# A mixer block with its input projection moved to the front and done by seven products per unit

## The chip, the cores and the metric

One core of one Trainium2 chip runs the whole program. The metric is the time of one execution in device microseconds. The core's engines are named as the profile names them: PE (TensorE, matrix products), PEld (its loading of stationary operands), DVE (VectorE), ACT (ScalarE), POOL (GpSimd) and SP (SyncE, which issues nearly all transfers here). Each engine takes its own instructions in order.

## What is computed

One layer of a decoder trunk on 1024 positions of 1024 features, in float32, batch 1. One projection `z = rms_norm(x) @ w_in` of 13312 columns feeds three branches and three gates; each branch has its own output projection, is multiplied by its gate, and the sum goes through `w_out` and then an MLP of 4096 features.

```python
h = rms_norm(x, g_mix)
rq, rk, rv, rg, dq, dk, dv, cq, gates = split_cols(h @ w_in, SPLITS)   # 1024,1024,2048,2048,1024,1024,1024,1024,3072
ret    = swish(rg) * head_norm(retention(rq, rk, rv), g_ret, True)     # 4 heads, chunks of 128
da     = head_norm(diff_attention(dq, dk, dv, lam), g_diff, False) * (1 - lam_init)   # 4 heads, two softmax maps
kv     = rms_norm(mem, g_mem) @ w_mem_kv                               # 256 memory tokens
ca     = memory_cross_attention(cq, kv)                                # 4 heads
g      = sigmoid(gates)
merged = g[0] * (ret @ w_ret_o) + g[1] * (da @ w_diff_o) + g[2] * (ca @ w_cross_o)
x = x + merged @ w_out
x = x + relu(rms_norm(x, g_ffn) @ w_up) ** 2 @ w_down
return rms_norm(x, g_final)
```

## The kernel before

Everything large lies with features on partitions and positions along the free axis, in two halves of 512 positions (`t` = 0, 1). Each operand of a product is kept as a high and a low part in float32r (`split`, lines 132 to 134: ACT casts, DVE subtracts), and `mm3` (lines 142 to 147) adds three matmuls for one product of blocks. `fm_gemm` (line 233) multiplies a block of 128 columns of a weight with one half of the normalised `hT`: 8 blocks of features, 24 matmuls of 512 columns, called a **half** here. Values are projected with positions on partitions, in tiles of 256 columns, 24 matmuls each.

The program goes through these stages, written one after another; a scheduler keeps each engine's order close to the written one. x comes in quarters, is normalised, and three gate blocks are multiplied on the way (`first_gemm`, line 330). Then memory keys and values (lines 377 to 399). Cross attention (lines 402 to 480) projects its queries head by head. Differential attention (lines 506 to 665) projects queries, keys and values of a head and then runs eight steps over blocks of 128 queries, from the longest (i = 7) to the shortest: scores (tile `dsc`), a DVE instruction that adds the bias and takes the maximum (`ds`, `dmx`), the exponential on ACT, a combination of the two maps on DVE, transposes on PE (`dtp`, copied to `dpt`), the product with the values (`do`), a norm and a store. Retention (lines 676 to 820) projects a head and runs eight chunks with a state (`Sf`, `Shl`), a score block (`rsc`), a transposed key block (`rkt`) and a centred norm (`rbs`, `rmv`, `on`).

The products that nothing waits for soon, 24 gate blocks and 16 blocks of `rg`, are cut into 80 halves; `fill(n)` emits n of them between steps: one after each step of differential attention (`FILL_D = 1`), in retention as `FILL_R` says (four halves a head in the first three heads, twelve in the last). Their results leave through an ACT copy (`spill`, tile `zg`) and a store to DRAM.

Then come the branch products. `branch` (line 857) first makes the operands of its four input pairs for both halves (`make`), then runs eight blocks of a weight over both halves; each half's result is multiplied by the sigmoid of its gate and added to `mg`. `make_ret` (line 895) makes retention's input: for each of a pair's two blocks the sigmoid of `rg` on ACT, a DVE product, a POOL product (line 911) and a split. Its raw tiles come from a ring of three, and a pair takes two of them (`rz`, `rin`). The order is cross, differential, retention in two parts. The output projection, the MLP and the last norm follow.

## Time and profile before

| | |
|---|---|
| median of three runs | 2728.25 us (2727.97 to 2728.79) |
| span of the profiled execution | 2726.0 us |
| PE busy | 2683.5 us, 98% |
| PEld, DVE, ACT, POOL busy | 84%, 45%, 31%, 5% |
| granted clock of PE | 0.998 on the mean |
| moved to and from DRAM | 219.54 MB, 81 GB/s on the mean |

The span runs from the first to the last instruction of the profiled execution; the times of the runs contain what lies around it as well. Busy time of PE is modelled from the starts of its matmuls. A matmul's own duration in a row is longer than the distance to the next one's start, since several are under way at once: what a matmul costs is the distance between starts. The same is true of DVE and ACT to a smaller degree, where an instruction starts shortly before the one ahead of it has ended.

### The profile page before, as it was taken

Reading aid. Unit: us, or ns where it says so; the run is one execution under the profiler, and the core shown is the slowest. Engines: PE = TensorE matmul, PEld = TensorE weight load, DVE = VectorE, ACT = ScalarE, POOL = GpSimd, SP = SyncE. Lnnn points to the kernel's source line nnn. Section 1 sums busy time; section 2 is a strip of 40 time slices with the busy share of each in tenths; the row PEclk is TensorE's granted clock in tenths of the full one; section 3 lists DMA queues with packets and bytes.
Section 4 is the critical chain, followed back from the end, with each engine's and each line's share of the span. In section 5 each row is a group of like instructions: output and inputs, shape, how many; then the busy total and the mean of one; then the engine's idle time right before and its main releaser. Section 6 shows DMA issues by size and latency. Waiting matters only on the chain. (4 is left out here: it accounts for less than half of the span.)

```text
span 2726.0 us, 33799 instructions
## 1 busy us (share of the span) xinstructions
PE 2683.5 (98%) x13858; PEld 2285.6 (84%) x13858; DVE 1220.2 (45%) x2217; ACT 839.1 (31%) x1549; POOL 129.1 (5%) x139
## 2 busy tenths in 40 slices
PE   6999999999999999999999999999999999999998
PEld 6988898888888888889898888878888888888887
DVE  7432243443435161533425436654564454544445
ACT  6332233232324242423233424332331212121222
POOL 3000000000001000000000002220000000000001
PEclk9999999999999999999999999999999999999999
DMA  4412112121212121111112635543421111111111
GB/s 161 157 63 78 62 48 75 47 80 51 80 47 70 45 66 55 63 55 55 62 55 82 206 127 189 180 160 97 132 85 47 47 47 54 44 57 47 47 39 62
DMA packets 99626, 219.54 MB, mean 81 GB/s; under 512 B 9488, under 2 KB 40208, under 8 KB 99472
## 3 DMA queue, kind: packets, MB, share of 16 engines
q1 hardware_dynamic: 99328, 217.36, 23.7%
q8 instruction: 108, 1.77, 0.3%
q14 instruction: 46, 0.38, 0.0%
q10 hardware_dynamic: 144, 0.03, 0.0%
HBM read 175.41 MB, written 41.94 MB: 80 GB/s over the span
## 5 line engine op out<-in xcount | busy, mean ns | idle before, releaser
L134 DVE TENSOR_TENSOR whl<-wst,whl 128x1024 fp32r<-128x1024 f32 x230 | 282.2, 1232 | 424.0 <-ACT whl L133 422.9
L133 ACT CAST whl<-wst 128x1024 fp32r<-128x1024 f32 x232 | 242.0, 1050 | 334.6 <-PE dn L147 254.2
L145 PE MATMUL zg<-hT,whl 128*128 128x512 f32 (+1 forms) x688 | 260.6, 382 | 3.9 <-ACT hT L133 3.8
L146 PE MATMUL zg<-hT,whl 128*128 128x512 f32 (+1 forms) x688 | 260.1, 379 | 0.8 <-DVE hT L134 0.8
L147 PE MATMUL zg<-hT,whl 128*128 128x512 f32 (+1 forms) x688 | 259.3, 378 | 0.0
L979 DVE TENSOR_TENSOR x<-x,dn 128x512 f32<-128x512 f32 (+1 forms) x248 | 164.6, 669 | 124.8 <-PE dn L147 124.7
L146 PE MATMUL dn<-u,whl 128*128 128x512 f32 (+1 forms) x544 | 205.3, 378 | 0.0
L147 PE MATMUL dn<-u,whl 128*128 128x512 f32 (+1 forms) x544 | 205.1, 377 | 0.0
L145 PE MATMUL dn<-u,whl 128*128 128x512 f32 (+1 forms) x544 | 205.1, 377 | 0.0
L147 PE MATMUL u<-h,whl 128*128 128x512 f32 x512 | 199.8, 390 | 0.0
L145 PE MATMUL u<-h,whl 128*128 128x512 f32 x512 | 199.3, 389 | 0.0
L146 PE MATMUL u<-h,whl 128*128 128x512 f32 x512 | 199.3, 389 | 0.0
L145 PEld LDWEIGHTS zg<-hT,whl 128*128 128x128 f32 x688 | 129.8, 190 | 26.5 <-ACT hT L133 5.7
L147 PEld LDWEIGHTS zg<-hT,whl 128*128 128x128 f32 x688 | 130.5, 190 | 22.5
L146 PEld LDWEIGHTS zg<-hT,whl 128*128 128x128 f32 x688 | 130.5, 190 | 22.2 <-DVE hT L134 1.4
L146 PE MATMUL rv<-whl,hT 128*128 128x256 f32 x512 | 145.0, 283 | 0.0
L147 PE MATMUL rv<-whl,hT 128*128 128x256 f32 x512 | 145.0, 283 | 0.0
L145 PE MATMUL rv<-whl,hT 128*128 128x256 f32 x512 | 145.0, 283 | 0.0
L957 DVE TENSOR_TENSOR ur<-ur 128x512 f32<-128x512 f32 x64 | 44.3, 692 | 193.1 <-ACT ur L956 193.1
L248 ACT COPY spill<-zg 128x512 f32<-128x512 f32 x80 | 47.0, 587 | 252.2 <-issue 131.5
L147 PEld LDWEIGHTS dn<-u,whl 128*128 128x128 f32 x544 | 102.4, 188 | 19.2 <-issue 0.2
L146 PEld LDWEIGHTS dn<-u,whl 128*128 128x128 f32 x544 | 102.4, 188 | 19.0 <-issue 0.2
(269 smaller groups left out, 5957.9 us busy)
## 6 DMA issues: line engine op xcount, KB each, us to landing
wst<-in_w_z SPq DMA_DIRECT2D x104, 512.0 KB, 3.5
g<-zg SPq DMA_DIRECT2D x64, 256.0 KB, 3.0
wst<-in_w_up SPq DMA_DIRECT2D x32, 512.0 KB, 3.4
wst<-in_w_down SPq DMA_DIRECT2D x32, 512.0 KB, 3.5
zg<-spill SPq DMA_DIRECT2D x48, 256.0 KB, 2.0
wst<-in_w_kv SPq DMA_DIRECT2D x16, 512.0 KB, 4.3
rn<-spill SPq DMA_DIRECT2D x64, 128.0 KB, 2.2
rg<-spill SPq DMA_DIRECT2D x32, 256.0 KB, 2.0
```

What stands on the lines that cost most here:

```text
L133: nc.scalar.copy(out=hl_hi, in_=src)
L134: eng.tensor_tensor(out=hl_lo, in0=src, in1=hl_hi.bitcast(F32), op=ALU.subtract)
L145: nc.tensor.matmul(out, ah, bh, start=first, stop=False)
L146: nc.tensor.matmul(out, ah, bl, start=False, stop=False)
L147: nc.tensor.matmul(out, al, bh, start=False, stop=last)
L248: nc.scalar.copy(out=st[:, :cols], in_=src_ps)
L957: nc.vector.tensor_tensor(out=r, in0=r, in1=r, op=ALU.mult)
L979: nc.vector.tensor_tensor(out=x2[d][t][:, cols], in0=x2[d][t][:, cols], in1=o[:, :width], op=ALU.add)
```

## The change

The whole projection is computed first, with fewer products, and goes through DRAM. It is done in 52 **units** of 256 columns (`unit_order`). Of a unit, the weight (features by columns) and the input (features by positions) are each cut into four quadrants: the two halves of the features, the two blocks of 128 columns, the two halves of the positions. `left_operands` forms three sums and differences of the weight's quadrants and one in place, and splits seven operands; the seven operands of the input (`hop`) are made once. `seven` then runs seven **quads** of 12 matmuls (four blocks of features, three matmuls each) where a block product by quadrants takes eight, and adds and reads out partial sums in between (`s1`, `s2`, `s3`, ACT copies from PSUM; results `zo`). Every result is stored to `z_d` in DRAM, features on partitions.

Memory keys and values are computed during the start and stored too. After the projection, cross attention runs without products in between and keeps its output in SBUF (`ac`); differential attention runs with the 16 halves of the cross branch product between its steps (four a head, after steps 7, 5, 3 and 1), retention with the 16 halves of the differential branch product, likewise. Each such half ends with a sigmoid on ACT, a DVE product and a store of the partial sum (`mg_d`); in retention the earlier sum is loaded and added on POOL. Queries and keys come from DRAM; values, now with features on partitions, are transposed on PE (`dvt`, `rvt`). The remaining two `branch` calls for retention come right after the retention steps.

```diff
-FILL_D = 1
-FILL_R = [[0, 1] * 4] * 3 + [[1, 2] * 4]
+FILL_D = [[1, 0] * 4] * 4
+FILL_R = [[1, 0] * 4] * 4
...
+    def left_operands(pool, src0, src1):
+        ra, rb = (pool.tile([P, 2, HALF], F32, tag="wr", name="wr", bufs=4) for _ in range(2))
+        nc.sync.dma_start(out=ra, in_=src0)
+        nc.sync.dma_start(out=rb, in_=src1)
+        s1, s2, s4 = (pool.tile([P, HALF], F32, tag="ws", name="ws", bufs=3) for _ in range(3))
+        add(s1, rb[:, 0], rb[:, 1])
+        add(s2, s1, ra[:, 0], ALU.subtract)
+        add(rb[:, 0], ra[:, 0], rb[:, 0], ALU.subtract)
+        add(s4, ra[:, 1], s2, ALU.subtract)
+        ops = {}
+        for key, src in (
+            ("11", ra[:, 0]), ("12", ra[:, 1]), ("2", s2), ("1", s1), ("3", rb[:, 0]), ("22", rb[:, 1]), ("4", s4)
+        ):
+            w = pool.tile([P, 2, HALF], F32R, tag="wo", name="wo", bufs=12)
+            split(w[:, 0], w[:, 1], src)
+            ops[key] = w
+        return ops
...
+        for i, u in enumerate(units):
+            w, x1, s1 = cur
+            more = i + 1 < len(units)
+            if more:
+                ws[units[i + 1]] = load(units[i + 1])
+            x2 = at_ps("x2")
+            quad(x2, w["12"], ops, B21)
+            emit(u, 0, 0, x2, s1)
+            quad(x1, w["2"], ops, T2, True)
+            s2 = tmp.tile([P, HALF], F32, tag="s2", name="s2", bufs=2)
+            nc.scalar.copy(out=s2, in_=x1)
+            x3 = at_ps("x3")
+            quad(x3, w["1"], ops, T1)
+            quad(x1, w["3"], ops, T3, True)
+            s3 = tmp.tile([P, HALF], F32, tag="s3", name="s3", bufs=2)
+            nc.scalar.copy(out=s3, in_=x1)
+            emit(u, 1, 1, x3, s3)
+            if more:
+                cur = begin(units[i + 1])
+            quad(x1, w["22"], ops, T4, True)
+            emit(u, 1, 0, x1, None)
+            quad(x3, w["4"], ops, B22, True)
+            emit(u, 0, 1, x3, s2)
...
+    seven(list(range(NU)), hop, lambda u: left_operands(wz, w_z[u, 0], w_z[u, 1]), zt, z_emit)
...
+    def branch_halves(b, w, w0, rhs, before):
+        for d in range(8):
+            hl = weight(w[w0 + d])
             for t in range(2):
+                o = fm_gemm(hl, rhs, t, HALF, "y")
+                g = zs_tile("sp", "g", 3)
+                nc.sync.dma_start(out=g, in_=gate_of(b * 8 + d, t))
+                nc.scalar.activation(out=g, in_=g, func=AF.Sigmoid)
+                add(g, o, g, ALU.mult)
+                if before:
+                    m = zs_tile("hf", "m")
+                    nc.sync.dma_start(out=m, in_=mg_d[d][t])
+                    nc.gpsimd.tensor_tensor(out=g, in0=g, in1=m, op=ALU.add)
+                nc.sync.dma_start(out=mg_d[d][t], in_=g)
+                yield
...
-            fill(FILL_D)
+            fill(FILL_D[h][7 - i])
...
+    def ad_load(t):
+        for k in range(KT):
+            raw = zs_tile("hf", "adr")
+            nc.sync.dma_start(out=raw, in_=da_d[k // 2][t][:, k % 2])
+            split(ad[k][t][:, 0], ad[k][t][:, 1], raw)
...
+        vt = at_ps("rvt")
+        for e in range(4):
+            nc.tensor.transpose(out=vt[:, e * P : (e + 1) * P], in_=vf[t][:, e, off : off + P], identity=ident)
         vhl = rp.tile([P, 2, HALF], F32R, tag="vhl", name="vhl")
-        split(vhl[:, 0], vhl[:, 1], vs[c])
+        split(vhl[:, 0], vhl[:, 1], vt)
...
-    branch(0, 2, w_co, 0, make_cross)
-    branch(1, 1, w_do, 0, make_diff)
     branch(2, 0, w_ro, 0, make_ret(0))
     branch(3, 0, w_ro, 8, make_ret(4))
```

How the order on an engine changes is shown at three places. The first is the projection on DVE. Before, at the projection of a differential head, its row of instructions is one subtraction for each weight block (`whl`) and the split of each result:

```order
L134 TENSOR_TENSOR whl<-wst,whl 128x1024
L138 SCALAR_TENSOR_TENSOR dq<-dq 128x512 x2
L134 TENSOR_TENSOR whl<-wst,whl 128x1024
L134 TENSOR_TENSOR dk<-dk 128x512 x2
L134 TENSOR_TENSOR whl<-wst,whl 128x1024
L134 TENSOR_TENSOR dv<-dv 128x256 x7
```

In the changed kernel, within a unit (`wr` raw quadrants, `ws` combined ones, `wo` split operands, `zo` results):

```order
L132 TENSOR_TENSOR wo<-wr,wo 128x512 x2
L149 TENSOR_TENSOR zo<-x_4688,s_4713 128x512
L132 TENSOR_TENSOR wo<-ws,wo 128x512
L149 TENSOR_TENSOR ws<-wr 128x512
L149 TENSOR_TENSOR wr<-wr 128x512
L132 TENSOR_TENSOR wo<-ws,wo 128x512
L149 TENSOR_TENSOR ws<-ws,wr 128x512
L132 TENSOR_TENSOR wo<-wr,wo 128x512
L149 TENSOR_TENSOR zo<-x_4688,s_4686 128x512
```

The work of one result is now spread over combinations, splits and sums, and the sums of a unit stand among the operands of the next.

The second place is ACT at the start of a differential head, steps 7 to 5. Before (`ds` are the exponentials, `don` the square of the norm, `spill<-zg` the copy that ends a half of fill):

```order
L588 ACTIVATE ds,dsm<-ds,dnm 128x1024 x2
L588 ACTIVATE ds,dsm<-ds,dnm 128x896
L133 CAST dpt<-dtp 128x512 x2
L588 ACTIVATE ds,dsm<-ds,dnm 128x896
L248 COPY spill<-dot 128x256
L248 COPY spill<-zg 128x512
L634 ACTIVATE don,dms<-do 128x256
L133 CAST dpt<-dtp 128x512
```

In the changed kernel (`g<-g` is the sigmoid of a gate):

```order
L662 ACT_TABLE_LOAD
L662 ACTIVATE ds,dsm<-ds,dnm 128x1024 x2
L662 ACTIVATE ds,dsm<-ds,dnm 128x896
L131 CAST dpt<-dtp 128x512 x2
L724 ACTIVATE spill<-dot,gdiff 128x128 x2
L662 ACTIVATE ds,dsm<-ds,dnm 128x896
L454 ACT_TABLE_LOAD
L454 ACTIVATE g<-g 128x512
L708 ACTIVATE don,dms<-do 128x256
```

A sigmoid has come where the copy of a half stood, with a table load before it and another before the next exponential.

The third place is DVE where the first inputs of the retention branch product are made (`rin`, `ar`). Before, they stand between the results (`g<-y,g`, `x<-x,g`) of the differential branch product:

```order
L903 SCALAR_TENSOR_TENSOR rin<-rin,vec,rsig 128x512 x2
L134 TENSOR_TENSOR ar<-rin,ar 128x512 x2
L870 TENSOR_TENSOR g<-y,g 128x512
L871 TENSOR_TENSOR x_0_1_13800<-x_0_1_13800,g 128x512
L134 TENSOR_TENSOR whl<-wst,whl 128x1024
L903 SCALAR_TENSOR_TENSOR rin<-rin,vec,rsig 128x512 x2
```

In the changed kernel they follow the norm of the last retention chunk (`on`):

```order
L859 TENSOR_SCALAR on<-ro,rmv,rvr_14868 128x512
L968 SCALAR_TENSOR_TENSOR rin<-rin,vec,rsig 128x512 x2
L132 TENSOR_TENSOR ar<-rin,ar 128x512 x2
L968 SCALAR_TENSOR_TENSOR rin<-rin,vec,rsig 128x512 x2
L132 TENSOR_TENSOR ar<-rin,ar 128x512 x2
L968 SCALAR_TENSOR_TENSOR rin<-rin,vec,rsig 128x512 x2
```

The first pairs now stand behind retention with no other product's results between them.

## Rows read from the trace of the kernel before

**Rows 1.** The page's first part: busy time, share of the span, instructions.

```profile
PE 2683.5 (98%) x13858; PEld 2285.6 (84%) x13858; DVE 1220.2 (45%) x2217; ACT 839.1 (31%) x1549; POOL 129.1 (5%) x139
```

**Rows 2.** Busy time by stage: stretch, us, engines (instructions), PE clock, DMA share, GB/s.

```profile
0.00:18.50 18.50, 2.21 (x6) 1.43 (x6) 9.04 (x11) 7.91 (x10) 6.59 (x10) 1.00 0.91 361
18.50:66.00 47.50, 43.33 (x312) 40.72 (x313) 39.73 (x99) 35.46 (x93) 14.38 (x20) 1.00 0.20 77
66.00:123.00 57.00, 57.00 (x434) 55.06 (x433) 28.61 (x38) 24.84 (x38) 0.00 (x0) 1.00 0.54 178
123.00:312.00 189.00, 188.25 (x945) 157.94 (x945) 62.05 (x122) 60.03 (x135) 0.00 (x0) 1.00 0.20 70
312.00:887.00 575.00, 573.94 (x3222) 498.35 (x3221) 235.76 (x631) 182.39 (x405) 27.82 (x32) 1.00 0.18 62
887.00:1560.00 673.00, 671.75 (x3817) 583.51 (x3816) 256.37 (x498) 216.22 (x403) 19.38 (x32) 1.00 0.22 73
1560.00:1734.00 174.00, 174.00 (x769) 144.16 (x768) 84.23 (x110) 60.95 (x92) 18.77 (x12) 1.00 0.48 160
1734.00:1917.00 183.00, 177.16 (x768) 144.44 (x767) 100.34 (x132) 63.81 (x100) 29.70 (x20) 0.99 0.44 141
1917.00:2726.00 809.00, 795.85 (x3600) 660.00 (x3598) 404.02 (x579) 187.53 (x276) 12.46 (x14) 0.99 0.17 58
```

**Rows 3.** The same for twelve 10 us stretches out of retention steps: first, and sum.

```profile
980.00:990.00 10.00, 10.00 (x50) 7.98 (x50) 9.65 (x23) 5.99 (x12) 0.54 (x1) 1.00 0.30 102
...
sum 120.00, PE 119.63 PEld 96.64 DVE 105.83 ACT 63.12 POOL 10.10; mean PE 9.97 PEld 8.05 DVE 8.82 ACT 5.26 POOL 0.84
```

**Rows 4.** Timeline of PE, matmuls of 256 columns: start, us, instruction.

```profile
976.36 0.28 PE L145 MATMUL rv<-whl,hT 128*128 128x256 f32 x1
976.48 0.28 PE L146 MATMUL rv<-whl,hT 128*128 128x256 f32 x1
```

**Rows 5.** Timeline of DVE in a differential step.

```profile
384.72 1.28 DVE L598 SCALAR_TENSOR_TENSOR ds<-ds,dr 128x1024 f32<-128x1024 f32 x1
385.92 0.68 DVE L569 CUSTOM_DVE_ANT_0 ds<-dsc,bias 128x512 f32<-128x512 f32 x1
386.53 0.08 DVE L569 DVE_READ_ACCUMULATOR2_ANT dmx<- 128x1 f32 x1
```

**Rows 6.** Timeline of ACT around its second table load.

```profile
1563.08 0.62 ACT L133 CAST ad<-din 128x512 fp32r<-128x512 f32 x1
1563.72 1.28 ACT L866 ACT_TABLE_LOAD   x1
1565.02 0.63 ACT L866 ACTIVATE g<-g 128x512 f32<-128x512 f32 x1
```

**Rows 7.** Timeline of PE around four transposes.

```profile
986.16 0.60 PE L801 MATMUL rot<-ident,on 128*128 128x128 f32 x4
986.51 0.48 PE L146 MATMUL zg<-hT,whl 128*128 128x512 f32 x1
```

**Rows 8.** Groups of DVE by shape: count, busy us, mean ns, idle before and releaser.

```profile
L134 DVE TENSOR_TENSOR whl<-wst,whl 128x1024 fp32r<-128x1024 f32 x230 | 282.2, 1232 | 424.0 <-ACT whl L133 422.9
L196 DVE SCALAR_TENSOR_TENSOR hf<-x,vec,rb 128x512 f32<-128x512 f32 x16 | 11.2, 742 | 2.4 <-PE rb L189 2.4
L134 DVE TENSOR_TENSOR dv<-dv 128x256 fp32r<-128x256 f32 x32 | 13.5, 423 | 60.9 <-ACT dv L133 60.9
```

**Rows 9.** Timeline of PE: last value matmul of retention head 0, first key matmuls after.

```profile
976.60 0.28 PE L147 MATMUL rv<-whl,hT 128*128 128x256 f32 x1
...
1033.59 0.39 PE L145 MATMUL rk<-hT,whl 128*128 128x512 f32 x1
...
1180.13 0.39 PE L145 MATMUL rk<-hT,whl 128*128 128x512 f32 x1
```

**Rows 10.** Timeline of POOL, pairs of products at line 911.

```profile
1659.00 2.85 POOL L911 TENSOR_TENSOR rin<-rin,rz 128x512 f32<-128x512 f32 x2 [4.31 <-DVE rin L903]
1666.64 2.85 POOL L911 TENSOR_TENSOR rin<-rin,rz 128x512 f32<-128x512 f32 x2 [4.79 <-DVE rin L903]
1673.68 2.85 POOL L911 TENSOR_TENSOR rin<-rin,rz 128x512 f32<-128x512 f32 x2 [4.20 <-DMA rin<-rn]
```

More of the change, by code (lines that the diff above doesn't have):

```diff
@@ L23 @@
 HALF = 512
-QT = 256
 NMEM = 256
@@ new lines, in quad, with seven, begin @@
+    def quad(out, w, ops, slot, again=False):
+        for kp in range(4):
+            sl = slice(kp * P, (kp + 1) * P)
+            o = ops[kp][slot]
+            mm3(
+                out,
+                (w[:, 0, sl], w[:, 1, sl]),
+                (o[:, 0], o[:, 1]),
+                kp == 0 and not again,
+                kp == 3,
+                again,
+            )
+    def seven(units, ops, load, tmp, emit):
+        def begin(u):
+            w = ws.pop(u)
+            x1 = mm_ps("x1")
+            quad(x1, w["11"], ops, B11)
+            s1 = tmp.tile([P, HALF], F32, tag="s1", name="s1", bufs=2)
+            nc.scalar.copy(out=s1, in_=x1)
+            return w, x1, s1
+        ws = {units[0]: load(units[0])}
+        cur = begin(units[0])
+        for i, u in enumerate(units):
[21 more added lines that the diff above has]
+            emit(u, 0, 1, x3, s2)
@@ L251, in hybrid_block @@
-    for j in range(24):
-        fillers.append((("f", GT + j * P), zg_d[j]))
-    for j in range(16):
-        fillers.append((("f", RG + j * P), [rg_d[j // 2][t][:, j % 2] for t in range(2)]))
-    def filler_halves():
-        while fillers:
-            key, dst = fillers.popleft()
-            hl = z_weight(key)
-            for t in range(2):
-                spill(dst[t], fm_gemm(hl, h_rhs, t, HALF, "zg"))
-                yield
-    halves = filler_halves()
-    def fill(n):
-        for _ in range(n):
-            next(halves, None)
@@ L364, in mem_hl @@
+    *_, acc = wide_sums(mt)
+    add(acc[:, :NMEM], acc[:, :NMEM], acc[:, NMEM:HALF])
+    rb = rms_finish(acc, NMEM)
+    mh = [sp0.tile([P, 2, HALF], F32R, name=f"mh{j}", tag=f"mh{j}") for j in range(4)]
     def mem_hl(k):
@@ L385, in mem_values @@
     def mem_values(h):
-        hls = [weight(w_kv[8 + 2 * h + j]) for j in range(2)]
+        hls = [kv_split(kv_load(w_kv[8 + 2 * h + j])) for j in range(2)]
         for m in range(2):
@@ L415, in cross_probs, with z_emit @@
-    def cross_probs(h, qs, t):
+        for _ in range(3):
+            next(xs, None)
+    for _ in xs:
+        pass
+    start.close()
+    zw = ExitStack()
+    wz = zw.enter_context(tc.tile_pool(name="wz", bufs=2, side="right", reuse_waits="tile"))
+    zt = zw.enter_context(tc.tile_pool(name="zt", bufs=2, side="right", reuse_waits="tile"))
+    def z_emit(u, n, t, a, b):
+        st = zt.tile([P, HALF], F32, tag="zo", name="zo", bufs=4)
+        if b is None:
+            nc.scalar.copy(out=st, in_=a)
+        else:
+            add(st, a, b)
+        nc.sync.dma_start(out=z_d[u][t][:, n], in_=st)
@@ new lines, in hybrid_block, with fill, drain, big @@
+    halves = iter(())
+    def fill(n):
+        for _ in range(n):
+            next(halves, None)
+    def drain():
+        for _ in halves:
+            pass
+    br = ExitStack()
+    bp = br.enter_context(tc.tile_pool(name="bp", bufs=1, reuse_waits="tile"))
+    ac = [[bp.tile([P, 2, HALF], F32R, name=f"ac{k}_{t}", tag=f"b{k}_{t}") for t in range(2)] for k in range(KT)]
+    cd = ExitStack()
+    cp = cd.enter_context(tc.tile_pool(name="cd", bufs=1, reuse_waits="tile"))
+    def big(name):
+        return cp.tile([P, 1024], F32, tag="s", name=name, bufs=4)
```

589 lines of the change are left out of this document (271 added, 318 removed).

## The prediction

> **What bounds the kernel now.** First the share of each engine: TensorE (PE) is busy 98% of the span, VectorE (DVE) 45%, ScalarE (ACT) 31% [rows 1]. Then the stretches, because that average mixes stages [rows 2]: PE is idle for 16 us before 18.5 us and for 4 us up to 66 us, then not at all until the retention branch product (6 us), and for 13 us in the tail; 42.5 us in all. So only fewer or cheaper matmuls can make it faster, and every stretch in which PE starts to wait is a loss. Third, how far the other engines are from being the bound where the change takes PE's work away: in twelve 10 us stretches out of the retention steps DVE is busy 105.83 of 120 us, 88%, beside a full PE [rows 3]. Everything below is in the time of the profiled execution, whose span is 2726.0 us; the median of the runs is 2728.25, so 2.25 us lie around it.
>
> **The projection.** Before, z has 3696 matmuls of 512 columns and 2592 of 256. Starts of the one lie 0.2266 us apart (174 us for the 768 of two branch products [rows 2]), of the other 0.12 [rows 4], so they take 837.5 + 311.0 = 1148.5 us of PE. After, 52 units of 7 quads of 12 matmuls are 4368 of 512 columns: 989.8 us. **PE loses 158.7 us.** A unit is 84 x 0.2266 = 19.0 us of PE. Beside it stand 14 DVE instructions of 512 elements at 0.61 us from start to start (the 512-element one from 385.92 to 386.53 in [rows 5]; each of those rows starts some 0.07 us before the one ahead ends), 8.6 us, some 11 ACT instructions of at most 0.62 us [rows 6], 6.8 us, and 2 MB through the queues, 110 GB/s, where the stretch 66 to 123 moved 178 GB/s with PE full [rows 2]. Each ACT copy that PE needs again (`s1`, `s2`, `s3`) has a quad, 2.7 us, before PE comes back to its bank; a copy and a cast before it are 1.2 us. I take the units as bound by PE; a miss there costs 52 times itself.
>
> Against it stand the transposes of the values, now feature-major: 64 in differential attention, 128 in retention. Four took from 986.16 to 986.51 [rows 7], and a foreign matmul that follows a group of them starts 0.1 us late: 192 x 0.088 + 48 x 0.1 = 22 us on PE. Net **-137 us of PE work**. The rest of PE's work moves only: 174 us of cross and differential branch product [rows 2] go between attention steps. Whether the 137 us remain depends on what PE waits for in five places.
>
> **1. Start.** z may not begin until x is normalised and all seven combinations are split. By the first result of a unit DVE has done 16 + 7 instructions of 1024 elements at 1.15, 73 of 512 at 0.61, 16 scalings at 0.66, and 20 small ones: 89 us at the pitch of [rows 5, 8] (each duration less 0.08). The stretch with the like work, 18.5 to 66, kept DVE 84% busy, and by 18.5 us it had done 9 us [rows 2]: first result at 18.5 + 80/0.84 = 114 us. PE has then done two quads (5.4 us); z ends at 114 + 984.4 = **1098 us**. Bound: at 90% DVE, 1091; with 5 us lost more, 1104.
>
> **2. Cross attention without fill.** The last stores of z wait in SP's queue ahead of the loads of queries, keys and values; some 2.8 MB at 361 GB/s (the first stretch of [rows 2]) are 8 us, with issue and first split 10 us in which PE stands. Then PE has 189 - 130.6 (24 of the old halves at 5.44) = 58 us, DVE some 63 (10 instructions of 1024 elements, 56 of 512, 32 of 256 and small ones). Nothing fills in, so DVE sets it at the 84% above: 75. Sum **85** (68 if PE were full, 95 at DVE 75%).
>
> **3. Differential attention.** Before, a head takes 575/4 = 143.75 us, of which PE spends 43.5 on eight halves of queries and keys (24 x 0.2266 = 5.44 each), 23.0 on eight tiles of values (24 x 0.12) and 43.5 on eight halves of fill: so 33.7 on attention itself. After, 33.7 + 1.8 transposes + 4 halves at 5.44 = 57.3 a head, **229 in all if PE stays full**. DVE: 235.76 less 40 weight splits at 1.15 and 31 for old inputs, plus 8 weight splits, 16 products with the gate at 0.61 and 29 for the new inputs: 207, 52 a head. Near enough to 57 that the pattern decides. In the four steps of a head without a half, PE has 15 us of its own and DVE some 23.5 (in step 6: scores 2.2, small ones 1.6, combination 1.8, transposed copies 1.1, and its share of the inputs), and the two meet only through the next half: 8 us of waiting a head, **262**. ACT gets 31 table loads at 1.28 us [rows 6], since the sigmoid of the gate and the exponentials alternate; they fall mostly in steps with a half, where PE has work. All of them on the path would be +40. Bounds 229 and 302.
>
> The row shows the load from 1563.72 to 1565.00 and the next ACT instruction at 1565.02: nothing follows the load. [...]
>
> **4. Retention.** A head's steps run from the last value matmul at 976.6 to the next head's first key matmul at 1033.59: 57 us with 4 halves, and the heads are 146.5 us apart [rows 9], PE full, DVE 88% [rows 3]. The change keeps 4 halves a head, so this row carries over: 57 + 3.5 transposes = 60.5, 242 for four. DVE grows by 2.5 us of gate products to 52.6: still under PE. Added in head 0: its first half waits until eight blocks of the differential output came through two buffers, cast and subtracted (some 1.8 us each, 14 us, of which PE can do half on scores), and 16 additions on POOL at 1.43 [rows 10] stand ahead of the small power that the output norm waits for. **256** (242 to 280), and 7 us before it, since its loads wait behind the masks, whose memory the last differential step holds.
>
> **5. Retention branch product.** Before, the first eight input pairs were made under the differential branch product, one pair each 7.4 us [rows 10], because a pair takes two of three raw buffers and the next load waits for one of them; only four waits of the second half remained (183 against 177.2 of PE). Now the first eight have no cover. 8 us to the first, 7 x 7.45 for the others: 60 us, in which PE can issue 84 of 384 matmuls; 300 x 0.2266 = 68; then 87 and 6 as before: **221**, +38. Bounds 205 and 230.
>
> Output projection, MLP and norm are as they were: 809 [rows 2].
>
> **The sum.** 1098 + 85 + 262 + 7 + 256 + 221 + 809 = 2738 us of span, 12 more than before; with 2.25 around it **2740**. In terms of PE: 2546 us of work instead of 2683.5, and 192 us of waiting instead of 42.5.
>
> **Rivals.**
> *Faster: the halves keep PE full.* Place: differential steps and the cross stage. If the matmuls of a half slide past the step's waits as they do before, where PE is full in every stretch of [rows 2], differential takes 232, cross 75, retention 245: 52 us less, **2688**. It decides where items 2 to 4 together (610 in my sum) fall under 598: then it is faster than before. For it: DVE's work is below PE's in both attentions. Against it: the old half needed nothing but PE and one ACT copy, and there were twice as many in differential steps.
> *Slower still: the table switches lie on the chain.* The exponentials that a step waits for are behind load, sigmoid and load on ACT (3.2 us). 31 x 1.28 on the path: **2778**. [...]
> *The units are not bound by PE.* If a copy or split comes late by 1.5 us in each unit: 52 x 1.5 = 78, **2818**. Against it: DVE and ACT would be 45% and 36% busy there, and the loads run a unit ahead.
>
> **How the numbers follow.** The forecast's case, waits in attention about as summed: 0.44, of which 0.34 slower by more than 0.2% and 0.10 within it (2722.8 to 2733.7, about what a measurement of this kernel can tell from no change). The faster rival and the way to it: 0.42, of which 0.36 faster and 0.06 within. Table switches 0.10, units 0.04, both slower. The forecast's own range is 2725 to 2765. The range for 8 in 10 runs from 2690 to 2800: one in ten below (a full PE with a quick start), one above. Faster 0.36, same 0.16, slower 0.48.
>
> **What would show it.** Right: matmuls of units 0.2266 apart from about 110 to 1098; PE busy some 65% in the cross stage, 85 to 90% in differential steps, with DVE above 78%; POOL pairs 7.4 us apart beside an idle PE at the start of the retention branch product. Wrong: the stretch of the units over 1000 us (units), ACT over 80% busy in differential steps with DVE waiting for the exponentials (switches), PE above 96% in attention (faster).

## The result

The changed kernel takes 2764.7 us (median; 2760.7 to 2767.5) where the kernel before takes 2728.5 beside it: a ratio of 1.0131, 95% interval 1.0116 to 1.0145. It is slower by 36 us; the forecast was 12 us slower. The sign was right and the time lies inside the range for 8 in 10 runs, but the size of the change was three times too small. The profiled execution has a span of 2765.7 us against the 2738 of the sum.

The first part of the page of the changed kernel (busy us, share of the span, instructions), beside [rows 1]:

```profile
PE 2610.9 (94%) x12126; PEld 2145.0 (78%) x12126; DVE 1567.6 (57%) x2749; ACT 998.0 (36%) x1803; POOL 127.2 (5%) x135
```

And its stretches, with the columns of [rows 2]: start, units, cross attention, differential attention, the gap before retention, retention, the first part and the rest of the retention branch product, output projection with MLP and norm.

```profile
0.00:95.50 95.50, 62.16 (x411) 57.74 (x411) 75.12 (x116) 50.98 (x77) 3.43 (x9) 0.94 0.51 178
95.50:1099.30 1003.80, 1003.10 (x4368) 822.14 (x4368) 491.88 (x727) 325.55 (x571) 0.00 (x0) 1.00 0.31 108
1099.30:1184.20 84.90, 62.99 (x373) 53.67 (x374) 66.57 (x133) 55.88 (x126) 0.00 (x0) 0.88 0.47 161
1184.20:1443.80 259.60, 237.95 (x1357) 197.50 (x1355) 193.95 (x577) 176.30 (x377) 26.19 (x31) 0.98 0.32 105
1443.80:1452.50 8.70, 0.88 (x3) 0.29 (x2) 0.64 (x2) 1.10 (x4) 0.54 (x1) 0.50 0.82 268
1452.50:1721.00 268.50, 250.84 (x1256) 203.89 (x1256) 217.33 (x465) 121.47 (x248) 38.40 (x48) 0.97 0.52 170
1721.00:1865.00 144.00, 110.69 (x423) 84.41 (x424) 75.94 (x97) 52.59 (x87) 43.75 (x30) 0.83 0.60 199
1865.00:1952.10 87.10, 81.88 (x347) 66.25 (x346) 43.16 (x59) 27.55 (x41) 2.48 (x2) 0.96 0.32 103
1952.10:2765.70 813.60, 800.37 (x3595) 659.15 (x3593) 403.06 (x577) 186.60 (x275) 12.44 (x14) 0.99 0.18 58
```

| term | forecast, us | measured, us | off by |
|---|---|---|---|
| start, to the first matmul of a unit | 108.6 | 95.5 | -13 |
| units | 989.8 | 1003.8 | +14 |
| cross attention | 85 | 84.9 | 0 |
| differential attention | 262 | 259.6 | -2 |
| gap before retention | 7 | 8.7 | +2 |
| retention | 256 | 268.5 | +12.5 |
| retention branch product | 221 | 231.1 | +10 |
| output projection, MLP, norm | 809 | 813.6 | +4.6 |
| span | 2738 | 2765.7 | +28 |

Two things stand out. In the units PE is full from end to end, in the last row it is idle for the same 13 us as before, and yet both are longer than summed: there the matmuls themselves got slower (in the units 228.9 ns from start to start on the mean, 226.7 in the kernel before). And PE's busy time is 2611 us where the forecast had 2546 of work, while its idle time is 155 us where the forecast had 192: what was missed is less waiting than work that took longer.

### The profile page after: what moved, and what is told of

The parts are those of the page before. It is cut to its first block, busy times and chain, and to the rows that moved or that the text cites. A ratio compares the mean times of both kernels' runs of the same rounds, so it can differ in the third digit from the quotient of the medians.

```text
span 2765.7 us, 32055 instructions
## 1 busy us (share of the span) xinstructions
PE 2610.9 (94%) x12126; PEld 2145.0 (78%) x12126; DVE 1567.6 (57%) x2749; ACT 998.0 (36%) x1803; POOL 127.2 (5%) x135
## 5 line engine op out<-in xcount | busy, mean ns | idle before, releaser
L144 PE MATMUL x<-hop,wo 128*128 128x512 f32 x1456 | 575.1, 395 | 6.0 <-ACT wo L131 5.3
L146 PE MATMUL x<-hop,wo 128*128 128x512 f32 x1456 | 571.7, 393 | 0.0
L145 PE MATMUL x<-hop,wo 128*128 128x512 f32 x1456 | 566.1, 389 | 0.0
L146 PEld LDWEIGHTS x<-hop,wo 128*128 128x128 f32 x1456 | 274.0, 188 | 64.4 <-DVE wo L132 0.2
L144 PEld LDWEIGHTS x<-hop,wo 128*128 128x128 f32 x1456 | 274.4, 188 | 61.0 <-ACT wo L131 5.5
L145 PEld LDWEIGHTS x<-hop,wo 128*128 128x128 f32 x1456 | 274.0, 188 | 61.3
L132 DVE TENSOR_TENSOR wo<-wr,wo 128x512 fp32r<-128x512 f32 x208 | 143.7, 692 | 238.6 <-ACT wo L131 238.6
L149 DVE TENSOR_TENSOR zo<-x,s 128x512 f32<-128x512 f32 x156 | 107.9, 692 | 243.2 <-PE x L146 127.7
L131 ACT CAST whl<-wst 128x1024 fp32r<-128x1024 f32 x112 | 115.8, 1047 | 336.3 <-PE dn L146 257.3
L131 ACT CAST wo<-wr 128x512 fp32r<-128x512 f32 x208 | 128.9, 622 | 165.6 <-PE x L146 161.9
L132 DVE TENSOR_TENSOR whl<-wst,whl 128x1024 fp32r<-128x1024 f32 x112 | 143.2, 1289 | 32.7 <-ACT whl L131 32.2
L144 PE MATMUL y<-ar,whl 128*128 128x512 f32 x256 | 105.8, 416 | 35.5 <-ACT ar L131 35.5
L131 ACT CAST wo<-ws 128x512 fp32r<-128x512 f32 x156 | 96.8, 622 | 110.0 <-PE x L146 106.3
L132 DVE TENSOR_TENSOR wo<-ws,wo 128x512 fp32r<-128x512 f32 x156 | 107.2, 689 | 27.1 <-ACT wo L131 27.0
```

The lines of the kernel that those rows point to most:

```text
L131: nc.scalar.copy(out=hl_hi, in_=src)
L132: eng.tensor_tensor(out=hl_lo, in0=src, in1=hl_hi.bitcast(F32), op=ALU.subtract)
L144: nc.tensor.matmul(out, ah, bh, start=first, stop=False, skip_group_check=again)
L145: nc.tensor.matmul(out, ah, bl, start=False, stop=False, skip_group_check=again)
L146: nc.tensor.matmul(out, al, bh, start=False, stop=last, skip_group_check=again)
L149: nc.vector.tensor_tensor(out=out, in0=a, in1=b, op=op)
```

## The experiments

Each run stands beside runs of the kernel before on the same chip; times are medians. The runs were made on four chips, on which the kernel before took 2728.4 to 2729.8 us, so times of different rows can be set side by side to about 1.5 us, besides their own scatter (7 us for the changed kernel).

| run | edit | us | ratio to before (95%) |
|---|---|---|---|
| e1_aligned | changed kernel, left pools 32 bytes up, right pools 32 bytes down | 2790.8 | 1.0225 (1.021 to 1.024) |
| e2_before_shifted | kernel before, all of SBUF 32 bytes on | 2729.8 | 1.0002 (0.9993 to 1.0011) |
| e3_tanh | gates of the early halves by tanh | 2742.5 | 1.0048 (1.0031 to 1.0064) |
| e4_ring7 | seven raw tiles instead of three | 2760.9 | 1.0135 (1.0104 to 1.0166) |
| e5_weights_512 | changed kernel, weights 480 bytes down | 2794.6 | 1.0239 (1.0223 to 1.0254) |
| e6_before_448 | kernel before, weights and all behind them 448 bytes on | 2729.2 | 1.0001 (0.9992 to 1.0011) |
| e7_gate_early | gates loaded a half earlier, both stages | 2780.4 | 1.0187 (1.0148 to 1.0225) |
| e8_all_four | e3, e4, e5 and e7 together | 2764.7 | 1.0129 (1.0112 to 1.0146) |
| e9_weights_with_operands | changed kernel, weights 448 bytes down | 2749.9 | 1.0075 (1.006 to 1.009) |
| e10_before_apart | kernel before, moving operands 32 bytes on | 2766.7 | 1.0139 (1.0122 to 1.0156) |
| e11_distance_tanh_ring | e9, e3 and e4 together | 2719.4 | 0.9963 (0.995 to 0.9976) |
| e12_no_fill | e9 without halves between the steps | 2798.2 | 1.0252 (1.0235 to 1.0269) |
| e13_gate_early_retention | e11, gates earlier in retention alone | 2715.3 | 0.9948 (0.9935 to 0.9962) |

### Why a full PE got slower

In the kernel before, 512-column matmuls started 226.7 ns apart in every stage where nothing else mixes with them. In the changed kernel the mean distance of 4351 starts in the units is 228.9 ns, in a pattern of three (the three matmuls of `mm3`): 231.7, 225.9, 229.2. The edit that the diff does not show: the weights now come from pools at the right end of SBUF (`side="right"`), the moving operands lie at the left, and each side has small tiles of its own, so that the two stand to one another at another distance in bytes than before. The places in bytes given from here on follow from the tiles and pools of the programs; a trace holds no addresses.

The first guess was the place of the operands modulo 64 bytes. e1 puts all of them on such a boundary (left 32 bytes up, right 32 bytes down), e2 takes the kernel before off it.

```diff
-    vec = const.tile([P, NV], F32, name="vec")
+    vec = const.tile([P, NV + 8], F32, name="vec")
...
+    edge = ctx.enter_context(tc.tile_pool(name="edge", bufs=1, side="right"))
+    pad = edge.tile([P, 8], F32, name="pad")
```

> The changed kernel with its tiles moved by 32 bytes, so that every operand of PE starts at a multiple of 64 bytes in SBUF as in the kernel before (in the changed kernel each starts 32 bytes past one); the order of instructions is the same, one small memset is added. Theory A, the address sets the distance of matmuls: starts 0.2267 us apart instead of 0.2291 in the units and 0.2283 in the MLP, 4368 x 0.0024 + 2640 x 0.0017 and some 3 us in the branch products, 18 us less, 2747. Rival, the distance comes from the traffic beside it or from the chip: distances and time stay, 2765.

> The kernel before with its tiles moved by 32 bytes past a multiple of 64, nothing else. Theory A: some 9500 matmuls of 512 columns, each 0.0017 to 0.0024 us later than now, 16 to 22 us more, 2745 to 2751, MLP distances 0.2283. Rival: 2728.5 and 0.2267.

Measured: e1 2790.8, 26 us slower than the changed kernel instead of faster, its units at 232.4 ns; e2 unchanged at 226.7 ns. The guess fell, but e1 showed that 32 bytes at either end move the time by 1%. The second guess was the place of the weights alone, modulo 512 bytes: e5 puts them on such a boundary with a pad of 480 bytes at the right end, e6 takes those of the kernel before off it.

> The changed kernel with only the tiles of the right end of SBUF (all weights but a quarter of those after the mixer) moved by 480 bytes, so that they start at a multiple of 512; all other tiles stay 32 bytes past one. In the changed kernel the weights start 480 bytes past a multiple and matmuls 0.2289 us apart, in the run with everything aligned to 64 they started 448 past and were 0.2324 apart, in the kernel before 0 or 32 past and 0.2267. Theory B, the place of the weights against 512 bytes sets the distance: 0.2267 in units and MLP, 4368 x 0.0022 + 3072 x 0.0017 and some 3 in the branch products, 18 us less, 2747. Rival, the two operands' distance from each other matters and 32 apart is no better: 0.2285 or more, 2760 or more.

> The kernel before with weights and all that lies behind them moved by 448 bytes, so that both operands of PE start 448 past a multiple of 512. Theory B: 0.2324 us from matmul to matmul, some 9500 x 0.0057 = 54 us more, 2783. Rival, only the two operands' places against each other matter: 0.2267 and 2729.

Measured: e5 2794.6, units at 233.3 ns; e6 unchanged. That guess fell too. What the runs had in common by then: where weights and moving operand stood at the same place modulo 2048 bytes (before, e2, e6) the distance was 226.7 ns; at 448 bytes apart (the changed kernel) 228.9, at 384 (e1) 232.4, at -32 (e5) 233.3. The other reading left was that the upper end of SBUF is slow. e9 and e10 tell them apart, one from each side.

```diff
 # e9: the changed kernel
+    edge = ctx.enter_context(tc.tile_pool(name="edge", bufs=1, side="right"))
+    pad = edge.tile([P, 112], F32, name="pad")
 # e10: the kernel before
     wp = ctx.enter_context(tc.tile_pool(name="wp", bufs=3))
+    low = ctx.enter_context(tc.tile_pool(name="low", bufs=1))
+    pad = low.tile([P, 8], F32, name="pad")
```

> The changed kernel with a pad of 448 bytes at the right end of SBUF: every weight pair moves down by 448 bytes, nothing else moves. Then the weights of the units stand at the same place as their moving operands modulo 4096 bytes, and the weights of the later stages at the same place modulo 2048. Theory C (the distance between weights and moving operand decides the spacing of the 512-column matmuls: 0 in the kernel before and in its two shifted runs gave 226.7 ns; 448 bytes in the changed kernel 228.9, 384 in e1 232.4, -32 in e5 233.3): spacing back to 226.7 ns in units, branch products and MLP, about 10 us less in the units and 9 in the later stages, 2746 in all. Theory D (weights at the upper end of SBUF are slow wherever they stand to the operand): spacing stays at 229 to 233 ns and the time at 2760 to 2795.

> The kernel before with a pad of 32 bytes behind the pool of the weights: the weights stay where they were, all moving operands stand 32 bytes further on (those weights of the MLP that take the fourth buffer move with them). Theory C: the distance is then -32 as in e5, and the 512-column matmuls stand about 233 ns apart instead of 226.7, except with that fourth buffer: some 10000 x 6.6 ns = 60 us or a bit more, about 2790. Theory D: the weights lie low as before, so no change, 2729.

Each of the next rows is a stretch with a full PE at full clock; the number behind PE's busy time counts its matmuls. First 400 us inside the units, of the changed kernel, of e5 and of e9, in that order:

```profile
500.00:900.00 400.00, 400.00 (x1749) 1.00 0.32 109
```

```profile
500.00:900.00 400.00, 400.00 (x1716) 1.00 0.31 108
```

```profile
500.00:900.00 400.00, 400.00 (x1767) 1.00 0.32 111
```

400 us by 1749, 1716 and 1767 are 228.7, 233.1 and 226.4 ns a matmul. And 500 us of the MLP, of the kernel before and of e10:

```profile
2100.00:2600.00 500.00, 500.00 (x2207) 414.12 (x2206) 241.46 (x327) 96.32 (x135) 0.00 (x0) 1.00 0.14 48
```

```profile
2100.00:2600.00 500.00, 500.00 (x2160) 404.67 (x2159) 234.00 (x314) 97.18 (x136) 0.00 (x0) 1.00 0.15 49
```

e9 gives back 14.8 us of the median: its units take 993.2 us (1003.8), its last stretch 808.0 (813.6). e10 makes the kernel before 37 us slower with a tile of 32 bytes, its gate blocks at 233.2 ns and its second MLP product at 233.2, although its weights lie low. So in these runs it was the distance between the two operands, not the end of SBUF.

e10 was expected at 2790: I had put 6.6 ns on some 10000 matmuls. They are 7368. From the branch products on, every fourth weight block lies in a buffer of its own (pool `wx`) behind the pad, and so moved along with the operands and kept the distance 0. That is why the mean in the branch and output products is 231.7 ns and in the first MLP product 230.2. It also makes e10 its own control: in the first MLP product halves of both kinds follow one another. First and last matmul of a half whose weights lie in one of the other three buffers, then of the next half, whose weights lie in the fourth:

```profile
2062.73 0.40 PE L145 MATMUL u<-h,whl 128*128 128x512 f32 x1
...
2068.10 0.39 PE L147 MATMUL u<-h,whl 128*128 128x512 f32 x1
2068.33 0.39 PE L145 MATMUL u<-h,whl 128*128 128x512 f32 x1
...
2073.54 0.39 PE L147 MATMUL u<-h,whl 128*128 128x512 f32 x1
```

23 distances take 5.37 and 5.21 us: 233.3 and 226.7 ns. Of the 63 halves of this product whose 24 matmuls stand together, 33 have 233 ns and 30 have 227; in the changed kernel, where the fourth buffer lies on the side of the operands, 33 have 229 and 30 have 227. 7368 x 6.6 ns are 49 us, and 37 were measured. Of this difference 4 us are the 256-column matmuls of the values, which got faster in e10 (118.3 ns from start to start for 120.0); the rest is open. So are the cause and the modulus: 0 and 2048 bytes gave the same 226.7 (units and MLP of e9), and 448, 384 and -32 are the only other distances that were run.

### What the table loads cost

e3 writes the sigmoid of the 32 early gates by a tanh; its trace has two table loads where the changed kernel has 32, and none among the exponentials. The missing factor of one half is put in where the retention branch is added.

```diff
-                nc.scalar.activation(out=g, in_=g, func=AF.Sigmoid)
-                add(g, o, g, ALU.mult)
+                nc.scalar.activation(out=g, in_=g, func=AF.Tanh, scale=0.5)
+                nc.vector.scalar_tensor_tensor(out=g, in0=g, scalar=1.0, in1=o, op0=ALU.add, op1=ALU.mult)
```

> The changed kernel with the gate of the 32 halves between attention steps made of a tanh, which needs no table load beside exponentials: 30 of the 32 loads go, 38.5 us of ACT; the number of other instructions is the same. Theory as predicted, the loads lie mostly where PE has a half to do: the differential stage falls from 260 by 0 to 10 us, time 2755 to 2765. Rival, they lie on the chain: 2727 to 2735.

Measured: 2742.5, 22 us less. The ACT groups of table loads in the changed kernel (count, busy us, mean ns, idle before):

```profile
L454 ACT ACT_TABLE_LOAD x16 | 20.5, 1283 | 0.8 <-DMA g<-z 0.5
L662 ACT ACT_TABLE_LOAD x14 | 18.0, 1283 | 4.2 <-DVE dnm L656 4.0
```

The stretch from the first score to the last output of differential attention, of the changed kernel and of e3:

```profile
1174.70:1443.80 269.10, 247.45 (x1404) 205.32 (x1402) 200.52 (x588) 181.18 (x387) 26.19 (x31) 0.98 0.32 103
```

```profile
1174.60:1423.70 249.10, 241.02 (x1402) 202.11 (x1402) 198.16 (x588) 144.15 (x358) 25.28 (x31) 0.99 0.35 112
```

ACT does 37 us less there, the stage gets 20 us shorter: so about half of the loads' own time (38.5 us) was on the path. Without them PE is busy 241 of 249 us.

### What the halves between steps are worth

e12 is e9 with both tables of halves at zero, so that the 16 halves of a stage are written behind its last head. The scheduler did not keep all of them there: of each 16, three ran among attention steps and 13 in one piece behind them.

```diff
-FILL_D = [[1, 0] * 4] * 4
-FILL_R = [[1, 0] * 4] * 4
+FILL_D = [[0] * 8] * 4
+FILL_R = [[0] * 8] * 4
```

> e9 with the two tables of halves all zero: no half of a branch product stands between the attention steps, all 16 of each stage follow its last head. Beside e9 (2749.9). Theory: the halves give PE work while the steps wait for VectorE. Without them the differential stage leaves PE some 151 us of work (238 less 16 halves x 5.44) and VectorE about 175, the retention stage 163 and 198; at the 88% to which VectorE was busy in such steps of the kernel before they take about 200 and 225, and the halves 87 us behind each: 287 + 312 against 260 + 267 in e9, so 2820, less some of the 20 us that the table loads cost: 2800 to 2820. Rival: the steps keep PE nearly as full alone and the halves between them only bring the table loads and the queue for the gate; then the stages take what their PE time is, and the loads fall away: 2730 to 2745.

Measured: 2798.2, 48 us more than e9 and just below the range of the theory. e12 in three stretches: the differential steps, with three halves of the cross branch product among them (72 of the 1092 matmuls); its other 13 halves; the retention steps, with three halves of the differential branch product:

```profile
1165.50:1408.00 242.50, 193.13 (x1092) 155.03 (x1092) 181.69 (x567) 130.36 (x339) 27.55 (x32) 0.92 0.22 69
1416.10:1489.80 73.70, 73.69 (x315) 60.88 (x316) 19.96 (x26) 17.80 (x26) 0.00 (x0) 0.96 0.64 217
1489.80:1688.00 198.20, 178.67 (x943) 137.53 (x941) 185.29 (x437) 106.22 (x219) 17.60 (x32) 0.99 0.37 122
```

In the differential steps PE is busy 80%, at a granted clock of 0.92 on the mean, DVE 75%. I had expected 200 us without any half: the steps leave even more idle than that, so the halves do fill PE there. In e9 the same stage with all 16 halves runs from 1166.6 to 1439.1 us, 30 us longer for 13 halves more, 71 us of PE; 41 fitted in, and of the 30 some 20 are the table loads (e3).

In retention they bought little. e9's steps with all 16 halves take 267 us, e12's with three of them 198: 69 us for 13 halves that are 71 us of PE, so next to nothing fitted in, and PE is busy 90% without them. (The first inputs of e12's steps came under the 13 cross halves, some us in its favour.) Up to the first matmul of the retention branch product both take 277 us (1445.0 to 1722.0 in e9, 1489.8 to 1766.7 in e12), since e12's halves cover the wait for that product's inputs; I had expected 312 for steps and halves. So 46 of the 49 us between the two spans arise between the first differential score and the retention steps, and 4 in the retention branch product.

### Retention, its gates and its branch product

At the boundary of two heads the load of a half's gate is issued only while its product runs (at 1580.33 us, the product's matmuls start from 1577.81 to 1583.17). On the queue of SP it stands behind stores and loads of the next head (issued from 1573.56 to 1579.09 us), and ACT waits for it until 1585.95 with the next head's casts behind it. ACT of the changed kernel there, and PE just behind (start, us, instruction, idle before and its releaser):

```profile
1578.97 0.62 ACT L131 CAST Shl<-Sf 128x512 fp32r<-128x512 f32 x1
1585.95 0.63 ACT L454 ACTIVATE g<-g 128x512 f32<-128x512 f32 x1 [6.37 <-DMA g<-z]
1586.49 1.03 ACT L131 CAST whl<-wst 128x1024 fp32r<-128x1024 f32 x1
1587.43 0.40 ACT L131 CAST qhl<-rq 128x256 fp32r<-128x256 f32 x1
```

```profile
1588.36 0.33 PE L791 MATMUL rvt<-ident,rvr 128*128 128x128 f32 x1 [1.20 <-ACT spill L869]
1591.05 1.22 PE L784 MATMUL rsc<-rq,rk 128*128 128x128 f32 x4 [2.35 <-DVE sf L786]
```

e7 loads each gate one half earlier into two tiles of its own, in both stages; e13 does it on top of e11 and in retention alone.

```diff
+        ahead = gate(0, 0)
         for d in range(8):
...
+                g = ahead
+                if (d, t) != (7, 1):
+                    ahead = gate(d + t, 1 - t)
                 o = fm_gemm(hl, rhs, t, HALF, "y")
-                g = zs_tile("sp", "g", 3)
-                nc.sync.dma_start(out=g, in_=gate_of(b * 8 + d, t))
```

> The changed kernel with the gate of a half between attention steps loaded one half earlier, into two tiles of its own. Theory, at the start of each retention head the gate's load stands behind 2.5 MB of the next head's inputs, the sigmoid that waits for it holds ACT's queue for 6 us, and PE runs out of work and drops to half clock: retention stage from 268 to 250 to 260, 8 to 18 us less, 2747 to 2757. Rival, the stage is held by DVE and the state: same 268, 2765.

> e11 with the gates of the retention stage's halves loaded one half earlier into two tiles of their own; those of the differential stage stay where they are. Beside e11 (2719.4). Theory: two of the waits at the heads' boundaries come from a gate that is queued behind the next head's inputs on SP; with it gone the retention stage loses the 5 us that it lost in e7, and the differential stage does not grow as it did there: 2713 to 2716. Rival: those waits are the next head's own inputs (the 5.4 us for rq in e11), which the gates ahead only push back; then no change, 2718 to 2722.

Measured, from the first score to the last transpose of retention: 268.1 us in the changed kernel, 263.3 in e7; 266.6 in e11, 261.1 in e13. PE's waits for `sf` at the score blocks fell from 5.6 us in e11 (5.5 in the changed kernel) to 1.8 in e13; its wait for the first `rq`, which the rival names, stayed (5.4 and 6.1 us). e7 as a whole was slower all the same: its differential stage grew from 269 to 280 us, at a granted clock of 0.96 instead of 0.98, with the cross halves emitted earlier (their last matmul at 1367 us instead of 1419). With the tanh in place of the sigmoid the same early gates do not lengthen that stage: from the first score to the last product it takes some 251 us in e8, 249 in e3. Why the times of e7 scatter (2769 to 2790) stays open. e13 is 4 us faster than e11, less than the 5.5 of the stage, and 1.3 of the 4 lie between the two chips.

e4 borrows four tiles for the raw inputs of the first eight pairs, where the change has three.

```diff
+        extra = [slots.pop() for _ in range(4)] if n == 2 else []
+        raws.extend(extra)
         at = [[a for j in range(4) for a in make(j, t)] for t in range(2)]
+        for i in extra:
+            raws.remove(i)
+            slots.append(i)
```

> The changed kernel with seven raw tiles instead of three while the first eight input pairs of the retention branch product are made. Theory, the ring of three sets the 7.3 us a pair: pairs 4 to 5 us apart, 57 us become 35, PE waits less and its clock comes back sooner: 18 to 25 us less, 2740 to 2747. Rival, the transfers (79% busy there) or POOL's 2.8 us a pair with DVE's wait behind it set it: under 6 us less, 2759 or more.

Measured: from the first matmul of the retention branch product to the first of the output projection 210 us instead of 221. The pairs come 5 us apart, as expected, but the 11 us are half of the 18 to 25 that I had drawn from it: the second half of the product got 4 us longer (102.4 instead of 98.6). The median of 2760.9 shows 4 us of the 11, with runs from 2754 to 2777; alone it is not told from the changed kernel. In e8 the four edits known by then gave 2764.7: its units ran at 233.3 ns by its e5 part, which ate what the others gave.

> The changed kernel with four of these edits: weights moved by 480 bytes, tanh for the gates between attention steps, seven raw tiles, gates loaded a half early. If they add up: 2764.7 - 18 - 22 - 11 - 12 = 2702, 1% faster than the kernel before. Rival, they hit the same waits: some 2720.

> The changed kernel with three edits together: the 448-byte pad, the gates of the 32 early halves by tanh (e3) and the seven raw tiles (e4). Theory C: 2764.7 - 22 (e3) - 4 to 11 (e4) - 19 (distance) = 2713 to 2720, faster than the kernel before by about 0.4%. Theory D: the pad gives nothing, 2732 to 2739 or more.

e11 takes 2719.4, as theory C had it, and e13 2715.3: with the distance mended, the tanh, the raw tiles and the earlier gates the changed order is **faster than the kernel before by 0.5%** (0.4 to 0.65). The page of e13, first part:

```profile
PE 2581.7 (95%) x12126; PEld 2134.3 (79%) x12126; DVE 1576.4 (58%) x2750; ACT 962.5 (36%) x1773; POOL 129.4 (5%) x135
```

## Why the prediction was right and wrong, point by point

The sign came out as forecast, and that PE paces the units and POOL's pairs the retention branch product. Three terms of the sum failed by their size: the distance of the matmuls (0.2266 us put in, 0.2289 measured in the units), retention, where a row was carried over (256 put in, 268.5 measured), and the retention branch product (221 put in, 231.1 measured). In differential attention two errors cancelled. And the sum had no term for the clock of PE.

**The projection.** Wrong in one term: 0.2266 us a matmul was read from the kernel before and carried over as if it belonged to the shape. In these runs it changed with where the operands lie: 226.7 to 233.3 ns for the one shape. 4368 x 2.2 ns are 9.6 of the 14 us missed in the units; e9, at the old distance, has 993.2. Some 3 more are the first six us of the units at half the clock (0.50; in e9 it was 4 us, a loss of 2): a stretch of 14.5 us at their start in the changed kernel, and PE's first matmuls there.

```profile
95.50:110.00 14.50, 14.50 (x51) 11.67 (x52) 14.46 (x24) 8.94 (x17) 0.00 (x0) 0.79 0.54 185
```

```profile
95.47 0.80 PE L144 MATMUL x<-hop,wo 128*128 128x512 f32 x1 [5.29 <-ACT wo L131]
96.07 0.63 PE L145 MATMUL x<-hop,wo 128*128 128x512 f32 x1
96.49 0.63 PE L146 MATMUL x<-hop,wo 128*128 128x512 f32 x1
```

That the units are bound by PE was right: 1003.1 of 1003.8 us busy. The forecast's own sign against it, a stretch of over 1000 us, did come, but not by its rival: in all 52 units PE waited for a copy once, for 0.7 us, and never for a split. The distance of the matmuls explains the last stretch too: +4.6 us, and 808.0 in e9.

**1. Start.** 13 us too long. I let PE stand until nearly all combinations were made; it begins with the first of them, and DVE makes the rest beside the first unit (14.46 of 14.5 us in the row above). z still ended at 1099 us against 1098, because this gain and the slower matmuls cancel.

**2. Cross attention.** Right in the sum: 84.9 (85), with 13 us of standing after the last matmul of z where I had 10, 72 us of the stage itself where I had 75, and PE 74% busy where I had 65%. The last 9.5 of the 84.9 us already hold scores of differential attention (the first starts at 1174.7), so only the sum of the two stages, 344.5 us where I had 347, is free of the choice of the border.

```profile
1098.88 0.39 PE L146 MATMUL x<-hop,wo 128*128 128x512 f32 x1
1112.40 0.58 PE L144 MATMUL csc<-mk,cq 128*128 128x256 f32 x1 [13.13 <-ACT cq L131]
```

**3. Differential attention.** 259.6 (262): the sum was right by luck, its parts were not. I had 33 us of waiting by the uneven pattern and nothing for the table loads. The loads cost 20 (e3); without them the stretch is 249 instead of 269, with PE busy 97% of it. The marks that the forecast had named for the stage were PE at 85 to 90% and DVE above 78%; it shows 92% and 75%. So two rivals were each true in part, with opposite signs: of the 40 us that the table switches would have cost, 20 came, and without them the stage would take some 240 us, nearer to the 232 of the faster rival (the halves keep PE full) than to my 262. That the halves fill PE in this stage is shown by e12 (41 of 71 us). The switch at 1230.45 cost ACT the load's 1.28 us and 0.03 us around it: the load starts 0.02 us after the end of the instruction ahead, and the next ACT instruction 0.01 us after the load's end.

```profile
1229.96 0.38 ACT L708 ACTIVATE don<-do 128x256 f32<-128x256 f32 x1 [0.20 <-PE do L146]
1230.24 0.19 ACT L708 ACTIVATION_READ_ACCUMULATOR don<-do 128x1 f32 x1
1230.45 1.28 ACT L454 ACT_TABLE_LOAD   x1
1231.74 0.63 ACT L454 ACTIVATE g<-g 128x512 f32<-128x512 f32 x1
```

**4. Retention.** 12.5 us too short, and the step that failed is "this row carries over": [rows 9] had fills that needed nothing but PE and a copy. The new half needs a gate from DRAM at its end, behind the next head's transfers on SP's queue; taking that away gives 5 us (e7, e13). Of the 12.5 us some 9 are work that took longer (PE busy 250.8 us, 242 forecast) and 4 are standing (17.7, 14 forecast). What made the work longer I can only read, not show: after its longer stops here PE worked at a granted clock of 0.50 for a while, its 512-column matmuls 0.43 us apart (from 1593.13 us, for one). The windows behind the start of the stage and behind the wait at 1588 us:

```profile
1450.00:1460.00 10.00, 7.25 (x31) 5.69 (x31) 4.81 (x12) 3.13 (x8) 0.00 (x0) 0.67 1.01 394
...
1590.00:1600.00 10.00, 8.96 (x35) 7.49 (x36) 7.01 (x18) 3.52 (x8) 0.54 (x1) 0.67 0.45 149
```

The stage's mean clock is 0.97. A clock of 0.67 on the mean of 10 us is 6.6 us at the lower level, 0.50, and a loss of at most 3.3; the mean of 0.97 over 268 us allows about 8, less where PE stood in that time, and the distance of the matmuls adds 0.8 (16 halves x 24 x 2.2 ns).

**5. Retention branch product.** The mechanism was right nearly to the number: pairs on POOL 7.1 to 7.3 us apart beside an idle PE (one gap was 8.2; 7.4 forecast), and 87 matmuls begun 60 us after the end of retention, where I had 84.

```profile
1728.66 2.88 POOL L976 TENSOR_TENSOR rin<-rin,rz 128x512 f32<-128x512 f32 x2 [9.88 <-DMA g<-z]
1735.87 2.79 POOL L976 TENSOR_TENSOR rin<-rin,rz 128x512 f32<-128x512 f32 x2 [4.33 <-DVE rin L968]
1743.08 2.79 POOL L976 TENSOR_TENSOR rin<-rin,rz 128x512 f32<-128x512 f32 x2 [4.42 <-DVE rin L968]
...
1780.15 2.80 POOL L976 TENSOR_TENSOR rin<-rin,rz 128x512 f32<-128x512 f32 x2 [4.31 <-DMA rin<-rn]
```

The 10 us missed are small sums: the 384 matmuls of the first half are done 132.5 us after the end of retention instead of 128, 2 of that because the first one starts after 10.0 us and not 8; the second half takes 98.6 instead of 93, since its first pairs come late, with 7.4 us of waits around 1865 us where [rows 2] had 6 in the whole stage, and matmuls 0.8 us long behind them (the granted clock reads 0.50 from 1871 to 1876):

```profile
1863.50 0.49 PE L144 MATMUL y<-ar,whl 128*128 128x512 f32 x1 [1.54 <-ACT ar L131]
1864.63 0.50 PE L145 MATMUL y<-ar,whl 128*128 128x512 f32 x1 [0.63 <-DVE ar L132]
1871.08 0.80 PE L144 MATMUL y<-ar,whl 128*128 128x512 f32 x1 [4.89 <-ACT ar L131]
1872.21 0.79 PE L145 MATMUL y<-ar,whl 128*128 128x512 f32 x1 [0.33 <-DVE ar L132]
```

**In sum**, of the 25 us between forecast and median 15 are the distance of the matmuls (e9); retention (12.5) and its branch product (10) are the rest, less the 13 that the start gave. The clock, which the sum left out, runs through several of these terms: PE was busy for 77 us at the lower clock (0.50), in the kernel before for 5. At 0.43 instead of 0.227 us from start to start that is some 34 us more of work, an estimate from these figures; no run takes it away by itself. Against it PE waited 37 us less than I had summed (155 and 192). That these two nearly cancel is luck.

## What to carry to other kernels

The distance of matmuls read from the trace held here only while the operands kept their relative place in memory: if an edit moves a pool, look up how far apart stationary and moving operand now lie (0 and 2048 bytes, with 226.7 ns, were the good distances of the five run here), and compare the count of matmuls in a stretch with a full PE before and after; a "busy" of 100% hides it (400.00 of 400 us at 1716 matmuls as at 1767). When fill work that needs only PE is exchanged for fill work that ends in a load or another function on ACT, cost what that load or function queues behind and what waits behind it, not only its own time (here 20 us for the tables and 5 for the gates). And a stop of PE had two prices in the changed kernel's trace, the stop itself and the lower clock behind it: after the 5.9 us up to 1452.5, another 4 us at 0.50.

## What the runs showed of the hardware that I had not expected

- The 512-column matmuls of float32r, each with its own weight load, started 226.7 ns apart where the weights and the moving operand stood at the same place modulo 2048 bytes in their partition (before, e2, e6, e9), and in the units 228.9, 232.4 and 233.3 ns apart at distances of 448 (the changed kernel), 384 (e1) and -32 bytes (e5), at a granted clock of 1.00 in all cases. Inside one product of e10 halves at 233 and 227 ns followed one another as the weights came from one buffer or another. A tile of 32 bytes made the kernel before 1.4% slower (e10). Why it is so stays open.
- In the changed kernel the granted clock read 0.50 while PE stood in the gap before retention (1443.8 to 1452.5 us) and for 4 us after it worked again, and 1.00 from 1457. The same followed other long stops: behind the 5.3 us ahead of the units it read 0.50 up to 101 us, behind the 4.9 us up to 1871.1 until 1876. 512-column matmuls then started 0.43 us apart. In the retention branch product, where PE had six matmuls for each pair, it stayed at 0.50 for the first three of these stretches and was back at 1.00 in the fifth:

```profile
1731.00:1741.00 10.00, 5.82 (x11) 3.50 (x12) 4.98 (x6) 5.51 (x10) 3.33 (x3) 0.50 0.68 221
1741.00:1751.00 10.00, 4.07 (x8) 1.84 (x7) 4.62 (x6) 2.30 (x4) 3.38 (x3) 0.50 0.75 260
1751.00:1761.00 10.00, 3.38 (x7) 1.87 (x7) 4.60 (x7) 3.05 (x6) 4.55 (x4) 0.50 0.79 263
1761.00:1771.00 10.00, 9.47 (x26) 6.46 (x27) 4.92 (x6) 4.37 (x8) 3.28 (x3) 0.69 0.65 211
1771.00:1781.00 10.00, 8.91 (x38) 6.60 (x36) 5.83 (x8) 2.30 (x4) 3.68 (x3) 1.00 0.55 173
```
